# A quarter of the weights' low parts summed by accumulating DMAs from GpSimd instead of by VectorE, in a fp32 streaming-encoder block

## The chip, the core and the metric

The kernel runs on one core of one Trainium2 chip. The metric is device time of one launch, in microseconds; lower is better. The change is to be judged against the median of the runs of the kernel before, 2222.36 us.

## The reference

One layer of a hybrid encoder on 256 tokens of width 2048, all in fp32. Cut to what matters, it is a row of large projections of a few tokens:

```python
h = rms_norm(x, g_mix)
cb, cc, cv, q, k, v, g, gate_conv, gate_ret = split(h @ w_in)      # 2048 x 22528
y_conv = (cb * causal_dwconv3(cc * cv)) @ w_conv_out               # 2048 x 2048
o = head_group_norm(retention(rotary(q), rotary(k), v))            # 8 heads, chunks of 64
y_ret = (silu(g) * o) @ w_ret_out                                  # 4096 x 2048
x = x + (sigmoid(gate_conv) * y_conv + sigmoid(gate_ret) * y_ret) @ w_o
a, b = split(rms_norm(x, g_ffn) @ w_ffn_in)                        # 2048 x 11264
x = x + (silu(a) * b) @ w_ffn_out                                  # 5632 x 2048
x = x + sigmoid(rms_norm(x, g_ple) @ w_ple_gate) * (p @ w_ple_proj)
out = rms_norm(x, g_final)
```

Every weight is read once, some 416 MB in all.

## The kernel before

All projections go through one function, `project`. It takes 512 output columns at a time, for both token tiles (2 x 128 tokens), and sums over the rows of the weight in blocks of 128. Four such blocks, a group, are one load of 1 MB into a buffer `raw` ([128, 4, 512] fp32; four buffers, loads issued from SyncE). The names say which projection it is: `cc`, `cv`, `cb` (convolution), `gc`, `gr` (gates), `co`, `qk`, `v`, `g` (retention, per head), `ro`, `wo`, `fa`, `fb`, `fo` (feed-forward), `pg`, `pp`. Nearly all have 16 blocks, so 4 groups; `ro` has 8 groups, `fo` 11, `pp` a half.

To keep fp32 accuracy with the faster fp32r format, each operand is split into a high part (the value rounded to fp32r) and a low part (what the rounding left). `split` (L186) does this for a group in two halves of two blocks each, h0 = 0 and h0 = 2. For a half, ScalarE casts the raw weights into `hi` (L191) and VectorE subtracts `hi` from the raw weights into `lo` (L192). `hi` and `lo` are rings of three buffers each, so the `hi` of a half can only be written when TensorE has done all products with the third half before it. `products` (L197) then issues three matmuls for each block and token tile: high x high (L200), high x weight's low (L201), low x weight's high (L202), so 12 matmuls of 512 columns for a half:

```python
hi, lo = (pool.tile([P, 2, W], F32R, tag=g, ...) for g, x in zip(tags, ("hi", "lo")))
last_copy[0] = nc.scalar.copy(out=hi, in_=raw[:, h0 : h0 + 2, :])
nc.vector.tensor_tensor(out=lo, in0=raw[:, h0 : h0 + 2, :], in1=hi.bitcast(F32), op=ALU.subtract)
```

After a projection, ScalarE or VectorE reads its two PSUM tiles, with the activation and the row scale (for instance `sa`, the sigmoid of `fa`). Transposes for the next stage are queued by `later`, to run inside a later projection. GpSimd does almost nothing: a power for each norm (L226). The order of the instructions on each engine is set by a scheduler when the program is built; on the chip each engine runs its own queue strictly in that order.

Of the kernel before, what the change touches and what calls it, by code (L numbers as in the profile page):

```python
# [11 lines left out]
F32 = mybir.dt.float32  # L12
# [17 lines left out]
KG = 4  # L30

# columns of the combined projection
C_B, C_C, C_V = 0, D, 2 * D
# [5 lines left out]

# rows of the stacked per-feature gains, columns once transposed  # L40
G_MIX, G_FFN, G_PLE, G_CONV, G_RET = 0, 16, 32, 48, 96


def shape_constants():
    """Rotary tables [S, 2, 128] and decay masks [HEADS, 128, 384]; they depend on shapes alone."""
    f32 = np.float32
    half = DK // 2
    inv = np.power(f32(ROPE_BASE), -np.arange(half, dtype=f32) / f32(half)).astype(f32)
    ang = np.arange(S, dtype=f32)[:, None] * inv[None, :]
    rope = np.stack([np.cos(ang), np.sin(ang)], axis=1).astype(f32)  # L50
    gamma = 1.0 - 2.0 ** (-5.0 - np.arange(HEADS))
    n, m = np.arange(S)[None, :], np.arange(S)[:, None]
    decay = np.power(gamma[:, None, None], np.abs(n - m)[None].astype(np.float64))
    decay = decay * (m // CHUNK <= n // CHUNK)[None] * DK**-0.5
    masks = np.concatenate([decay[:, :P, :P], decay[:, :P, :]], axis=2).astype(f32)
    return np.ascontiguousarray(rope), np.ascontiguousarray(masks)
# [3 lines left out]
def block_kernel(  # L60
# [25 lines left out]
    const = ctx.enter_context(tc.tile_pool(name="const", bufs=1))  # L86
    blk_pool = ctx.enter_context(tc.tile_pool(name="blk", bufs=36))
    raw_pool = ctx.enter_context(tc.tile_pool(name="raw", bufs=4))
    split_pool = ctx.enter_context(tc.tile_pool(name="split", bufs=3))
    small = ctx.enter_context(tc.tile_pool(name="small", bufs=2))  # L90
    ps_mm = ctx.enter_context(tc.tile_pool(name="ps_mm", bufs=4, space=PSUM))
# [10 lines left out]

    # Work that waits for a later point of the stream of projections, so that TensorE finds its inputs ready.
    waiting = []
# [10 lines left out]

# [1 line left out]
    gains = const.tile([P, P], F32, name="gains")  # L117
# [6 lines left out]
    nc.vector.memset(minus_half, -0.5)  # L124
    # the activation table's load and TensorE's clock ramp, ahead of the data
    warm = small.tile([P, NT], F32, name="warm", bufs=1)
# [5 lines left out]
    def transposed(src, j0, name):  # L132
        """PSUM [P, 2, S]: column blocks j0 and j0 + 1 of src [P tokens, NT, ...], transposed."""
        pt = aux(name)
        for t in range(NT):
            for j in range(2):
                nc.tensor.transpose(
                    out=pt[:, j, t * P : (t + 1) * P],
                    in_=src[:, t, (j0 + j) * P : (j0 + j + 1) * P],
                    identity=ident,  # L140
                )
        return pt

    def transposed_split(src, name, gain=None, wide=W):
        """src [P tokens, NT, wide] -> high and low parts of its transpose, [P, wide // P, S] each."""
        nk = wide // P
        hi = blk([P, nk, S], F32R, f"{name}_hi")
        lo = blk([P, nk, S], F32R, f"{name}_lo")
        for j0 in range(0, nk, 2):
            pt = transposed(src, j0, f"{name}_t{j0}")  # L150
            if gain is None:
                nc.scalar.copy(out=hi[:, j0 : j0 + 2, :], in_=pt)
                nc.vector.tensor_tensor(
                    out=lo[:, j0 : j0 + 2, :], in0=pt, in1=hi[:, j0 : j0 + 2, :].bitcast(F32), op=ALU.subtract
                )
            else:
                for j in range(2):
                    g = gains[:, gain + j0 + j : gain + j0 + j + 1]
                    nc.scalar.activation(out=hi[:, j0 + j, :], in_=pt[:, j, :], func=AF.Copy, scale=g)
                    nc.vector.scalar_tensor_tensor(  # L160
                        out=lo[:, j0 + j, :],
                        in0=pt[:, j, :],
                        scalar=g,
                        in1=hi[:, j0 + j, :].bitcast(F32),
                        op0=ALU.mult,
                        op1=ALU.subtract,
                    )
        return [(hi[:, j, :], lo[:, j, :]) for j in range(nk)]

    def load(pieces, k0, kn, name, step=KG):  # L170
        """kn row blocks, from row k0 * P on, of the pieces' columns, side by side."""
        raw = raw_pool.tile([P, KG, W], F32, tag="raw", name=f"{name}_raw")
        for j in range(0, kn, step):
            at, jn = 0, min(step, kn - j)
            for w, c0, cn in pieces:
                nc.sync.dma_start(
                    out=raw[:, j : j + jn, at : at + cn],
                    in_=w[(k0 + j) * P : (k0 + j + jn) * P, c0 : c0 + cn].rearrange("(c p) n -> p c n", p=P),
                )
                at += cn  # L180
        return raw

    last_copy = [None]

    def split(raw, kn, name, pool=split_pool):
        """High and low parts of kn loaded row blocks."""  # L186
        parts = []
        for h0 in range(0, kn, 2):
            tags = ("hi", "lo") if pool is split_pool else ("blk", "blk")
            hi, lo = (pool.tile([P, 2, W], F32R, tag=g, name=f"{name}_{x}{h0}") for g, x in zip(tags, ("hi", "lo")))  # L190
# [5 lines left out]
    def products(ps, left, right, t, first, last):  # L196
        """ps += left^T @ right for token tile t, from high and low parts."""  # L197
        (xh, xl), (wh, wl) = left, right
# [5 lines left out]
    def project(lhs, nk, pieces, name, loaded=None, before=None):  # L204
        """PSUM tiles [P tokens, W], one per token tile: lhs^T @ (the pieces' columns, side by side)."""
        ps = [ps_mm.tile([P, W], F32, tag="mm", name=f"{name}_ps{t}") for t in range(NT)]
        for k0 in range(0, nk, KG):
# [3 lines left out]
            raw = load(pieces, k0, kn, name) if loaded is None else loaded[k0 // KG]  # L211
            parts = split(raw, kn, name)
            for j in range(kn):
# [5 lines left out]
    def rsqrt(r, var, scale, name, bias=EPS):  # L219
        """r = (var * scale + bias) ** -0.5: GpSimd's power, then a Newton step."""  # L220
        n = r.shape[1]
# [13 lines left out]
    class RowScale:  # L235
        """1 / rms of rows given in column chunks [P, NT, <= W]."""

# [21 lines left out]
        def so_far(self, t, n):  # L259
            """Mean square of the first n chunks of token tile t, plus EPS."""  # L260
            s = small.tile([P, 1], F32, tag="part", name="part")
# [4 lines left out]
        def done_with(self, t, n, s):  # L266
            """The scale of token tile t, from what so_far gave and chunk n, the last."""
            rsqrt(self.r[:, t : t + 1], self.parts[:, t, n : n + 1], 1.0 / D, "rms", bias=s)
            return self.r[:, t : t + 1]

# [1 line left out]
    hT = []  # L272
# [42 lines left out]

# [1 line left out]
    ycT = []  # L317
# [71 lines left out]

# [1 line left out]
    yrT = []  # L391

    def scores(h, qkT, mask):
        """High and low parts of the decayed scores, [P, 3 * P]: keys 1 with queries 1, keys 0 with queries 0 and 1."""
        sc = aux(f"sc{h}")
# [18 lines left out]
    def mix_values(h, ph, pl, vh, vl, on):  # L414
        """on = GroupNorm(scores @ v), without its gain."""
        o_ps = []
        stats = small.tile([P, NT, 2], F32, tag="stats", name=f"stats{h}")
        # (block of the scores, token tile of the keys) for the queries of each token tile
        for t, blocks in enumerate((((1, 0),), ((2, 0), (0, 1)))):
# [88 lines left out]

# [1 line left out]
    mT = []  # L510
# [11 lines left out]

# [1 line left out]
    x1, h2T = [], []  # L524
# [15 lines left out]

# [1 line left out]
    aT = []  # L542
# [38 lines left out]

# [1 line left out]
    x3 = []  # L583
# [21 lines left out]

    # the last chunk goes one token tile after the other, so that the first one's norm and store are hidden,
    # and in halves, so that little is left after the last product
    gf = blk([P, W], F32, f"gf{last}")
# [33 lines left out]
    "g_ffn", "w_ffn_in", "w_ffn_out", "g_ple", "w_ple_gate", "w_ple_proj", "g_final",  # L642
]  # fmt: skip

# [20 lines left out]
```

## Time and profile before

| what | us |
|---|---|
| runs, median of 2 (lowest, highest) | 2222.36 (2222.16, 2222.55) |
| the profiled execution: its span, first to last instruction | 2220.6 |
| TensorE busy | 2205.8 |
| VectorE busy | 1222.5 |
| ScalarE busy | 975.4 |
| GpSimd busy | 9.4 |

For the profiled execution the page gives its span and no other time; the median of the runs is 1.8 us above that span. Busy time is summed over the instructions of an engine. The engines run side by side, so the time of the kernel is that of the longest chain of instructions that wait for one another, not a sum over the engines.

### The profile page before, as it was taken

The page shows a single profiled execution, that of the slowest core. Times are in us where ns is not written, and L with a number is a line of the kernel's source. Part 1 is how long each engine was busy: PE and PEld are TensorE (multiplying, and loading weights), DVE is VectorE, ACT ScalarE, POOL GpSimd, SP SyncE. Part 2 cuts the span into 40 slices and gives each one's busy share as a digit, 9 for nine tenths or more (in the row PEclk, how much of TensorE's full clock was granted, in tenths as well). Part 3 has the DMA queues.
Part 4 walks back from the last instruction along what each step waited for, and adds up shares of the span by engine and source line. Part 5 has one row for each costly group of instructions (what it writes and reads, how often), then busy time and mean ns, then how long its engine had stood idle before and what let it go on. Part 6 is the DMA issues. An engine that isn't in the chain of part 4 may idle for free.

```text
span 2220.6 us, 24771 instructions
## 1 busy us (share of the span) xinstructions
PE 2205.8 (99%) x10054; PEld 1834.0 (83%) x10054; DVE 1222.5 (55%) x1347; ACT 975.4 (44%) x1101; POOL 9.4 (0%) x19
## 2 busy tenths in 40 slices
PE   9999999999999999999999999999999999999998
PEld 7888888888888888888888888888888888888887
DVE  5555544444666665666655555555555555444465
ACT  5444444444444444444443345444444444444454
POOL 0000000000000000000000000000000000000000
PEclk9999999999999999999999999999999999999999
DMA  7555555555555555555555565555555555555553
GB/s 263 187 189 190 189 189 190 195 199 193 174 190 182 181 179 186 178 178 180 177 190 189 190 209 205 185 190 192 191 184 191 191 190 183 196 194 191 191 195 128
DMA packets 229106, 420.05 MB, mean 189 GB/s; under 512 B 7424, under 2 KB 42368, under 8 KB 228992
## 3 DMA queue, kind: packets, MB, share of 16 engines
q1 hardware_dynamic: 228992, 418.48, 55.2%
q8 instruction: 78, 1.28, 0.2%
q14 instruction: 36, 0.29, 0.0%
HBM read 416.35 MB, written 2.10 MB: 188 GB/s over the span
## 4 chain that ended last, share of the span: by engine, by line
PE 99%; DMA 0%; ACT 0%; issue 0%; DVE 0%; SPq 0%; ACTq 0%; POOLq 0%
PE fo_ps L201 4%; PE fa_ps L202 4%; PE fa_ps L201 4%; PE fa_ps L200 4%; PE fo_ps L202 4%; PE fb_ps L200 4%; PE fo_ps L200 4%; PE fb_ps L202 4%; PE fb_ps L201 4%; PE v_ps L202 3%; PE v_ps L201 3%; PE v_ps L200 3%; PE g_ps L202 3%; PE g_ps L201 3%; PE g_ps L200 3%; PE qk_ps L201 3%
## 5 line engine op out<-in xcount | busy, mean ns | idle before, releaser
L192 DVE TENSOR_TENSOR fo_lo<-fo_raw,fo_hi 128x1024 fp32r<-128x1024 f32 x88 | 107.8, 1225 | 123.5 <-ACT fo_hi L191 123.5
L192 DVE TENSOR_TENSOR fa_lo<-fa_raw,fa_hi 128x1024 fp32r<-128x1024 f32 x88 | 107.8, 1225 | 111.4 <-ACT fa_hi L191 111.4
L192 DVE TENSOR_TENSOR fb_lo<-fb_raw,fb_hi 128x1024 fp32r<-128x1024 f32 x88 | 107.8, 1225 | 110.8 <-ACT fb_hi L191 110.8
L191 ACT CAST fa_hi<-fa_raw 128x1024 fp32r<-128x1024 f32 x88 | 92.8, 1054 | 142.8 <-PE fa_ps L202 87.9
L191 ACT CAST fo_hi<-fo_raw 128x1024 fp32r<-128x1024 f32 x88 | 92.8, 1055 | 137.4 <-PE fo_ps L202 132.4
L191 ACT CAST fb_hi<-fb_raw 128x1024 fp32r<-128x1024 f32 x88 | 92.7, 1053 | 121.9 <-PE fb_ps L202 85.3
L201 PE MATMUL fo_ps<-fo_lo,aT_hi 128*128 128x512 f32 x352 | 137.1, 389 | 0.0
L202 PE MATMUL fa_ps<-fa_hi,h2T_lo 128*128 128x512 f32 x352 | 137.0, 389 | 0.0
L201 PE MATMUL fa_ps<-fa_lo,h2T_hi 128*128 128x512 f32 x352 | 137.0, 389 | 0.0
L202 PE MATMUL fo_ps<-fo_hi,aT_lo 128*128 128x512 f32 x352 | 137.0, 389 | 0.0
L201 PE MATMUL fb_ps<-fb_lo,h2T_hi 128*128 128x512 f32 x352 | 136.9, 389 | 0.0
L202 PE MATMUL fb_ps<-fb_hi,h2T_lo 128*128 128x512 f32 x352 | 136.9, 389 | 0.0
L200 PE MATMUL fa_ps<-fa_hi,h2T_hi 128*128 128x512 f32 x352 | 127.2, 392 | 0.0
L200 PE MATMUL fo_ps<-fo_hi,aT_hi 128*128 128x512 f32 x352 | 124.4, 390 | 0.0
L192 DVE TENSOR_TENSOR ro_lo<-ro_raw,ro_hi 128x1024 fp32r<-128x1024 f32 x64 | 78.4, 1225 | 83.0 <-ACT ro_hi L191 83.0
L200 PE MATMUL fb_ps<-fb_hi,h2T_hi 128*128 128x512 f32 x352 | 122.6, 389 | 0.0
L191 ACT CAST g_hi<-g_raw 128x1024 fp32r<-128x1024 f32 x64 | 67.2, 1050 | 109.8 <-PE g_ps L202 81.9
L191 ACT CAST v_hi<-v_raw 128x1024 fp32r<-128x1024 f32 x64 | 67.4, 1054 | 106.3 <-PE v_ps L202 53.3
L192 DVE TENSOR_TENSOR v_lo<-v_raw,v_hi 128x1024 fp32r<-128x1024 f32 x64 | 78.3, 1224 | 62.4 <-ACT v_hi L191 62.4
L191 ACT CAST ro_hi<-ro_raw 128x1024 fp32r<-128x1024 f32 x64 | 67.5, 1054 | 102.3 <-PE ro_ps L202 98.9
L192 DVE TENSOR_TENSOR qk_lo<-qk_raw,qk_hi 128x1024 fp32r<-128x1024 f32 x64 | 78.3, 1224 | 61.0 <-ACT qk_hi L191 61.0
L192 DVE TENSOR_TENSOR g_lo<-g_raw,g_hi 128x1024 fp32r<-128x1024 f32 x64 | 78.3, 1224 | 60.4 <-ACT g_hi L191 60.4
(241 smaller groups left out, 5467.9 us busy)
## 6 DMA issues: line engine op xcount, KB each, us to landing
fa_raw<-in_w_ffn_in_dram SPq DMA_DIRECT2D x44, 1024.0 KB, 4.9
fb_raw<-in_w_ffn_in_dram SPq DMA_DIRECT2D x44, 1024.0 KB, 4.9
fo_raw<-in_w_ffn_out_dram SPq DMA_DIRECT2D x44, 1024.0 KB, 5.0
qk_raw<-in_w_in_dram SPq DMA_DIRECT2D x64, 512.0 KB, 4.3
v_raw<-in_w_in_dram SPq DMA_DIRECT2D x32, 1024.0 KB, 5.0
g_raw<-in_w_in_dram SPq DMA_DIRECT2D x32, 1024.0 KB, 4.8
ro_raw<-in_w_ret_out_dram SPq DMA_DIRECT2D x32, 1024.0 KB, 5.0
cv_raw<-in_w_in_dram SPq DMA_DIRECT2D x16, 1024.0 KB, 4.9
```

The source lines that it names most:

```text
L191: last_copy[0] = nc.scalar.copy(out=hi, in_=raw[:, h0 : h0 + 2, :])
L192: nc.vector.tensor_tensor(out=lo, in0=raw[:, h0 : h0 + 2, :], in1=hi.bitcast(F32), op=ALU.subtract)
L200: nc.tensor.matmul(out=ps, lhsT=xh[:, ts], rhs=wh, start=first, stop=False)
L201: nc.tensor.matmul(out=ps, lhsT=xh[:, ts], rhs=wl, start=False, stop=False)
L202: nc.tensor.matmul(out=ps, lhsT=xl[:, ts], rhs=wh, start=False, stop=last)
```

## The change

In every second group of a projection (the 2nd, 4th, ...), the second half's low part no longer comes from VectorE. ScalarE casts the high part as before, then writes its negative into a buffer `rest` (a ring of three of its own), and a DMA issued on GpSimd adds the raw weights onto it in place, from SBUF to SBUF, 512 KB each. `rest` then stands where `lo` stood. There are 190 such halves. The pool `blk`, which holds activations, goes from 36 buffers to 34 to make room. Comments are taken out as well, which moves line numbers: L191 and L192 become L201 and L202, L194 to L196 are new, and the matmuls L200 to L202 become L210 to L212.

```diff
-    blk_pool = ctx.enter_context(tc.tile_pool(name="blk", bufs=36))
+    blk_pool = ctx.enter_context(tc.tile_pool(name="blk", bufs=34))
     raw_pool = ctx.enter_context(tc.tile_pool(name="raw", bufs=4))
     split_pool = ctx.enter_context(tc.tile_pool(name="split", bufs=3))
+    rest_pool = ctx.enter_context(tc.tile_pool(name="rest", bufs=3))
...
-    def split(raw, kn, name, pool=split_pool):
+    def split(raw, kn, name, pool=split_pool, by_dma=False):
         parts = []
         for h0 in range(0, kn, 2):
+            if pool is split_pool and h0 == 2 and by_dma:
+                hi = pool.tile([P, 2, W], F32R, tag="hi", name=f"{name}_hi{h0}")
+                lo = rest_pool.tile([P, 2, W], F32R, tag="rest", name=f"{name}_rest{h0}")
+                last_copy[0] = nc.scalar.copy(out=hi, in_=raw[:, h0 : h0 + 2, :])
+                nc.scalar.activation(out=lo, in_=hi.bitcast(F32), func=AF.Copy, scale=-1.0)
+                nc.gpsimd.dma_start(out=lo, in_=raw[:, h0 : h0 + 2, :], accum_op=ALU.add)
+                parts += [(hi[:, j, :], lo[:, j, :]) for j in range(2)]
+                continue
...
-            parts = split(raw, kn, name)
+            parts = split(raw, kn, name, by_dma=k0 // KG % 2 == 1)
```

The scheduler also orders the engines' queues anew. On TensorE, at the seam between projection `fa1` and the next one, `fb1`, the queue before reads (`fa1_hi2` and `fa1_lo2` are the last half of `fa1`):

```order
L200 MATMUL fa1_ps1_10200<-fa1_hi2_10325,h2T3_hi_9916 128x512
L201 MATMUL fa1_ps1_10200<-fa1_lo2_10326,h2T3_hi_9916 128x512
L202 MATMUL fa1_ps1_10200<-fa1_hi2_10325,h2T3_lo_9917 128x512
L200 MATMUL fb1_ps0_10358<-fb1_hi0_10362,h2T0_hi_9417 128x512
L200 MATMUL fb1_ps1_10359<-fb1_hi0_10362,h2T0_hi_9417 128x512
```

`fa1` is finished before `fb1` begins. In the changed kernel, the same place on TensorE starts so (`fa1_rest2` is the low part that the DMA sums):

```order
L212 MATMUL fa1_ps1_10327<-fa1_hi0_10449,h2T3_lo_10040 128x512
L210 MATMUL fa1_ps0_10326<-fa1_hi2_10453,h2T3_hi_10039 128x512
L210 MATMUL fa1_ps1_10327<-fa1_hi2_10453,h2T3_hi_10039 128x512
L210 MATMUL fb1_ps0_10487<-fb1_hi0_10491,h2T0_hi_9534 128x512
L210 MATMUL fb1_ps1_10488<-fb1_hi0_10491,h2T0_hi_9534 128x512
```

Only the two matmuls of `fa1`'s last half that need no low part stand here; then the 12 of `fb1`'s first half follow. Still on TensorE in the changed kernel, after those 12:

```order
L211 MATMUL fb1_ps1_10488<-fb1_lo0_10492,h2T0_hi_9534 128x512
L212 MATMUL fb1_ps1_10488<-fb1_hi0_10491,h2T0_lo_9535 128x512
L211 MATMUL fa1_ps0_10326<-fa1_rest2_10454,h2T3_hi_10039 128x512
L212 MATMUL fa1_ps0_10326<-fa1_hi2_10453,h2T3_lo_10040 128x512
L211 MATMUL fa1_ps1_10327<-fa1_rest2_10454,h2T3_hi_10039 128x512
```

The other 10 matmuls of `fa1`'s last half have moved behind the first half of `fb1`. On ScalarE, the queue at the start of `fb1` before (`sa1` is the reading of `fa1`'s two PSUM tiles):

```order
L191 CAST fb1_hi0_10362<-fb1_raw_10360 128x1024
L191 CAST fb1_hi2_10366<-fb1_raw_10360 128x1024
L553 ACTIVATE sa1_10353<-fa1_ps0_10199,r2_r_9219 128x512
L553 ACTIVATE sa1_10353<-fa1_ps1_10200,r2_r_9219 128x512
L191 CAST fb1_hi0_10396<-fb1_raw_10394 128x1024
L191 CAST fb1_hi2_10400<-fb1_raw_10394 128x1024
```

The two readings stand between the first and the second group. On ScalarE in the changed kernel, the same two groups:

```order
L201 CAST fb1_hi0_10491<-fb1_raw_10489 128x1024
L201 CAST fb1_hi2_10495<-fb1_raw_10489 128x1024
L201 CAST fb1_hi0_10525<-fb1_raw_10523 128x1024
L563 ACTIVATE sa1_10482<-fa1_ps0_10326,r2_r_9334 128x512
L563 ACTIVATE sa1_10482<-fa1_ps1_10327,r2_r_9334 128x512
L194 CAST fb1_hi2_10529<-fb1_raw_10523 128x1024
L195 ACTIVATE fb1_rest2_10530<-fb1_hi2_10529 128x1024
```

The readings have moved one cast later, directly ahead of the cast and the negation of the half whose low part a DMA sums. GpSimd's queue in the feed-forward now holds nothing but these DMAs, two for each projection of four groups.

## Rows read from the trace of the kernel before

**Rows 1.** The page: span, then busy time of each engine, share, instructions.

```profile
span 2220.6 us, 24771 instructions
...
PE 2205.8 (99%) x10054; PEld 1834.0 (83%) x10054; DVE 1222.5 (55%) x1347; ACT 975.4 (44%) x1101; POOL 9.4 (0%) x19
```

**Rows 2.** The page: the chain of work that ended last, by engine.

```profile
PE 99%; DMA 0%; ACT 0%; issue 0%; DVE 0%; SPq 0%; ACTq 0%; POOLq 0%
```

**Rows 3.** Busy time by stretch: the start, the feed-forward's middle, the end.

```profile
core 0: us, PE busy (x) PEld busy (x) DVE busy (x) ACT busy (x) POOL busy (x), PEclk, DMA share, GB/s
0.00:100.00 100.00, 94.47 (x431) 78.44 (x432) 54.91 (x78) 51.84 (x75) 1.41 (x7) 0.97 0.66 228
1500.00:1800.00 300.00, 300.00 (x1354) 249.02 (x1353) 158.51 (x149) 128.20 (x134) 0.00 (x0) 1.00 0.55 189
2100.00:2221.00 121.00, 111.32 (x585) 95.91 (x583) 67.76 (x92) 56.69 (x80) 1.79 (x3) 0.98 0.48 165
```

**Rows 4.** Who waited for whom: us in total, times, longest us.

```profile
ACT fo_hi L191 <- PE fo_ps L202: 132.4, 82, 1.7
DVE fo_lo L192 <- ACT fo_hi L191: 123.5, 88, 1.5
```

**Rows 5.** Timeline around one hand-over, 1600.6 to 1604 us: PE, ACT, DVE.

```profile
start us, us, engine line op out<-in xcount [idle before <-releaser]
1600.70 0.39 PE L202 MATMUL fb_ps<-fb_hi,h2T_lo 128*128 128x512 f32 x1
1600.93 0.62 PE L200 MATMUL fa_ps<-fa_hi,h2T_hi 128*128 128x512 f32 x2
1601.13 1.06 ACT L191 CAST fa_hi<-fa_raw 128x1024 fp32r<-128x1024 f32 x1 [1.67 <-PE fb_ps L202]
1602.22 1.22 DVE L192 TENSOR_TENSOR fa_lo<-fa_raw,fa_hi 128x1024 fp32r<-128x1024 f32 x1 [0.18 <-ACT fa_hi L191]
1603.42 0.39 PE L202 MATMUL fa_ps<-fa_hi,h2T_lo 128*128 128x512 f32 x1
1603.65 0.62 PE L200 MATMUL fa_ps<-fa_hi,h2T_hi 128*128 128x512 f32 x2
1603.85 1.05 ACT L191 CAST fa_hi<-fa_raw 128x1024 fp32r<-128x1024 f32 x1 [1.66 <-PE fa_ps L202]
```

**Rows 6.** Instruction groups by form, ScalarE: count, busy us, mean ns, idle before.

```profile
L191 ACT CAST fo_hi<-fo_raw 128x1024 fp32r<-128x1024 f32 x88 | 92.8, 1055 | 137.4 <-PE fo_ps L202 132.4 <-PE fb_ps L202 5.0
...
L553 ACT ACTIVATE sa<-fa_ps,r_r 128x512 f32<-128x512 f32 x22 | 15.1, 690 | 10.8 <-PE fa_ps L202 10.8
...
L347 ACT CAST ych<-y 128x512 fp32r<-128x512 f32 x8 | 4.9, 622 | 0.4
...
L635 ACT ACTIVATE x<-x,r_r 128x512 f32<-128x512 f32 x4 | 2.7, 715 | 2.8 <-DVE r_r L233 2.8
```

**Rows 7.** The page's costliest groups: the subtraction on VectorE.

```profile
L192 DVE TENSOR_TENSOR fo_lo<-fo_raw,fo_hi 128x1024 fp32r<-128x1024 f32 x88 | 107.8, 1225 | 123.5 <-ACT fo_hi L191 123.5
```

**Rows 8.** DMA issues: count, KB each, median us from issue to landing.

```profile
fa_raw<-in_w_ffn_in_dram SPq DMA_DIRECT2D x44, 1024.0 KB, 4.9
...
cc_raw<-in_w_in_dram SPq DMA_DIRECT2D x8, 512.0 KB, 9.8
res<-in_x_dram SPq DMA_DIRECT2D x4, 512.0 KB, 6.0
pp_raw<-in_w_ple_proj_dram SPq DMA_DIRECT2D x4, 512.0 KB, 3.6
...
mix_in<-in_g_mix_dram SPq DMA_DIRECT2D x1, 8.0 KB, 1.7
```

## The prediction

> **What bounds the kernel now.** I read the page's busy times first: TensorE is busy 2205.8 of 2220.6 us, VectorE 1222.5, ScalarE 975.4 [rows 1]. The chain that ended last is 99% TensorE [rows 2], and by stretch TensorE has no gap at all in the middle (300.00 of 300 us at granted clock 1.00); its 14.8 us of idle time lie at the start and the end [rows 3]. So the kernel is bound by its matmuls. VectorE and ScalarE run ahead and then wait for TensorE to free a `hi` buffer: 82 of the 88 casts of `fo` wait for that, 1.7 us at most, and the subtraction waits for the cast [rows 4]. Taking work from VectorE shortens nothing on the path. It can only show where TensorE was idle, so even a perfect result is worth less than 14.8 us, 0.7%; what a measurement of this kernel tells from no change is about 2%, 44 us. The question is whether the new way of making a low part is ready in time, since from a TensorE that never waits, each wait is added to the end in full.
>
> How much time is there? The timeline of one hand-over shows it [rows 5]. Twelve matmuls, one half, take 1603.65 - 1600.93 = 2.72 us, 0.2265 each. The last matmul with an old half starts at 1600.70, its slot ends at 1600.93; the cast starts 0.20 later, takes 1.06, the subtraction starts 0.03 later and takes 1.22. So a low part is there 0.20 + 1.06 + 0.03 + 1.22 = 2.5 us after its buffer came free. TensorE wants it two halves and two matmuls later, 26 x 0.2265 = 5.9 us: 3.4 us to spare now.
>
> **The change part by part.**
>
> *Removed:* 190 subtractions of 1.225 us [rows 7], 233 us of VectorE. All of it lies beside TensorE's work: worth nothing.
>
> *Added on ScalarE:* 190 negations of 1024 columns. No row has one. The cast of that size takes 1.055; a scaled copy of 512 columns takes 0.715 against 0.622 for a cast of 512 from the same memory [rows 6]. So between 1.05 and 2 x 0.715 = 1.43; I take the cast plus the difference, 1.15. That is 219 us on an engine with 1245 us free, again nothing in sum, but each stands in the chain of its low part.
>
> *Added:* 190 accumulating DMAs of 512 KB. Call L the time from the issue on GpSimd to the landing that TensorE waits for. The chain is now 0.20 + 1.06 + 0.03 + 1.15 + 0.03 = 2.5 us, and then L. Each place has its own slack for L:
> - At the end of a projection the scheduler puts the first half of the next one in front (shown in the order of the change): 38 matmuls instead of 26, 8.6 us, slack 6.1. The 77 projections of four groups and the four `ro` end so: 81 places.
> - The other 109 are inside projections. Where nothing else is ahead on ScalarE the slack is 5.9 - 2.5 = 3.4: 64 places (`fo`, most of `ro`, `fa`, `v`, `g`, `cb`).
> - The half moved behind the next projection's first half frees its buffer late. In the next four-group projection ScalarE's queue has the cast that needs this buffer ahead of the cast for the DMA, so the count begins there: 3.4 - 1.06 = 2.3. I count 22 such places (`qk`, `cc`, `gc`, `wo`, `pg`).
> - Where ScalarE also reads the finished PSUM tiles in between, two of 0.69 us [rows 6], 2.3 - 1.4 leaves 1.0: 23 places (`fb`, `gr`, `co`, `cv`), as the order of ScalarE shows for `fb1`.
>
> A wait in one place does not shorten the next, since the count starts from TensorE's own progress. So the added time is 81 (L - 6.1) + 64 (L - 3.4) + 22 (L - 2.3) + 23 (L - 1.0), each term only where it is positive.
>
> *L.* The trace has no DMA from GpSimd, none that adds and none inside SBUF. Below: a plain load of 512 KB lands 3.6 us after its issue (`pp_raw`), and 8 KB, almost no data, takes 1.7. Above: 512 KB among a pile of loads at the start takes 9.8 (`cc_raw`), and `res`, 512 KB issued into the stream, 6.0 [rows 8]. An adding DMA must read both operands, 1 MB in all, and 1 MB lands in 4.9 (`fa_raw`, rows 8). The weight stream also goes on: it holds the DMA engines for 0.55 of the time [rows 3], that is 0.55 x 5.44 = 3.0 us for each group of 5.44, and a DMA that comes at any moment shares with it for about 0.55 x 3.0 = 1.6 us. I take 4.9 + 1.6 = 6.5, near the row of `res`, and keep 3.6 and 9.8 as ends. The descriptor work on GpSimd has no row; it is inside this spread.
>
> The Trainium skill speaks against the change here. Its page "Collectives: The Full Stack", section "The bandwidth ceiling: the fold count and why AG ≠ RS ≠ AR", says that a reduction in a DMA reads two sources through one read ring and so runs at half the rate of a copy. No row here shows an adding DMA; by that rule the plain 3.6 us is no fair price, and the sum would be the one made from the 1 MB row.
>
> Sum at L = 6.5: 81 x 0.4 = 32, 64 x 3.1 = 198, 22 x 4.2 = 92, 23 x 5.5 = 127, together 450 us. On the profiled execution that is 2220.6 + 450 = 2670.6; the median of the runs lies 1.8 above the span, so **2672 us**, 20% slower. At L = 3.6 the sum is 101 and the time 2324; at 9.8 it is 1077 and 3299.
>
> *Edits that I cost at nothing.* The raw buffer of every second group is held until the DMA has read it, so its next load starts later; there are four buffers, 21.8 us of TensorE work, for a load of 4.9 us, and if a stall of 6 us is added it still lands in time. VectorE's other work comes earlier, not later. `blk` loses two of 36 buffers; they are needed only where heads and gates are all held, late in the retention, and a shortage would cost waits of a few us there. The DMAs share GpSimd's queue with 13 powers that wait for VectorE; one DMA stands behind each, and if it came late that is 13 waits of a few us at most. Stalls leave TensorE idle in short gaps; at the start, where it idles 5.5 of 100 us, the granted clock is 0.97 [rows 3], so I price no clock loss.
>
> **The rivals.**
>
> *Quick as a plain copy* (L between 2.6 and 4.3). If adding costs no more than copying and the stream does not disturb it, L is 3.6 and the time 2324. For it: the DMA engines are idle 45% of the time, and nothing goes to HBM. Against: `res` took 6.0 for the same bytes. The Trainium skill, page "DMA: Bandwidth & Descriptors", section "Anatomy of one DMA — SWDGE (gpsimd) path", fits 2.0 us plus bytes over 436 GB/s, an estimate of 3.2 us for 512 KB, which would give 70 us and 2293; it is a fit for copies, and no run here shows it.
>
> *Hidden* (not slower). Where L is 2.6 or less the sum is 22 x 0.3 + 23 x 1.6 = 43 us, within 2%; at 2.3 it is 30 us, 2252. It needs an adding DMA of 512 KB to beat every load of that size in the trace by a us, against a floor of 1.7 for 8 KB. TensorE's waits in the `fb` places would then be the only ones.
>
> *The DMA becomes the bound* (L over 8.5). If the adding path is slow in the DMA engines, or GpSimd takes microseconds to issue, all 190 waits lengthen together, 190 us for each us of L: 3052 at 8.5, 3299 at 9.8, and beyond that the weight loads come late too. For it: nothing in the trace shows the rate of adding. Against: 45% of the DMA time is free.
>
> **How the numbers follow.** Forecast, L from 4.3 to 8.5: 0.72. Quick copy: 0.11. DMA as the bound: 0.13. Hidden: 0.04, of which 0.01 for a gain over 2%, which needs an unseen saving on TensorE. The range goes from L = 3.6 to L = 8.5, 2324 to 3052, and I write 2325 to 3050; it leaves out some 0.07 below and 0.13 above. Slower by over 2%: 0.95, within: 0.04, faster: 0.01.
>
> **What would show it.** TensorE's waits should name the DMA of `rest`, in about 190 places, with L read as issue to landing near 6.5; TensorE's busy time should stay near 2200 while the span grows; VectorE should fall by 233 us and ScalarE rise by 219. The waits at the seams (81) should be under 1 us and those in `fb` and `gr` the longest, near 5.5. The forecast is wrong if L is under 4.3, if waits name loads or `lo` instead, or if the longer time comes with longer matmuls or a lower clock.

## The result and the profile after

The changed kernel takes 2401.05 us (two runs, 2399.01 and 2403.08) against 2222.36: a ratio of 1.0805, 95% interval 1.0773 to 1.0836. It is slower, as forecast, and inside the range, but by 179 us and not by 450. The profiled execution grew from a span of 2220.6 to 2401.3 us, 180.7 us.

The page of the changed kernel, against [rows 1] and [rows 2]:

```profile
span 2401.3 us, 25606 instructions
...
PE 2257.7 (94%) x10054; PEld 1843.6 (77%) x10054; DVE 996.2 (41%) x1157; ACT 1173.1 (49%) x1291; POOL 176.8 (7%) x209
...
q0 software_dynamic: 27360, 99.63, 22.0%
...
issue 81%; PE 12%; DMA 4%; ACT 1%; POOL 1%; DVE 1%; POOLq 0%; SPq 0%; ACTq 0%
```

VectorE fell by 226 us and ScalarE rose by 198, both beside the path. TensorE's idle time went from 14.8 to 2401.3 - 2257.7 = 143.6 us, 129 more, and its busy time rose by 52. These two are the whole 181 us. Do not read the chain here: 81% of it is put down to "issue", time in which the engine waited for nothing that the profile shows. The waits name the cause at once.

The waits of TensorE in the changed kernel (us in total, times, longest), where the kernel before had none in the stream:

```profile
PE fo_ps L211 <- DMA fo_rest<-fo_raw: 21.6, 19, 1.3
PE fb_ps L211 <- DMA fb_rest<-fb_raw: 20.4, 11, 2.1
PE ro_ps L211 <- DMA ro_rest<-ro_raw: 14.6, 12, 1.9
PE qk_ps L211 <- DMA qk_rest<-qk_raw: 12.4, 8, 2.3
PE co_ps L211 <- DMA co_rest<-co_raw: 7.7, 4, 2.2
PE gr_ps L211 <- DMA gr_rest<-gr_raw: 7.4, 4, 1.9
PE fa_ps L211 <- DMA fa_rest<-fa_raw: 7.0, 11, 1.9
PE cv_ps L211 <- DMA cv_rest<-cv_raw: 6.7, 4, 1.8
PE v_ps L211 <- DMA v_rest<-v_raw: 6.6, 8, 1.8
```

All rows of waits for `rest`, fourteen, are together 127 us in 100 waits. None of TensorE's waits names a load. `fa`, `fb`, `qk` and `v` have two DMAs in each projection, but wait in only half as many places: 11 of 22, 11 of 22, 8 of 16, 8 of 16. The half at the seam, moved behind the next projection's first half, does not wait.

One wait of `fb`, in the timeline of the changed kernel (start, duration, engine):

```profile
1696.89 1.05 ACT L201 CAST fb_hi<-fb_raw 128x1024 fp32r<-128x1024 f32 x1 [2.12 <-PE fb_ps L212]
...
1698.48 1.37 ACT L563 ACTIVATE sa<-fa_ps,r_r 128x512 f32<-128x512 f32 x2 [0.53 <-PE fa_ps L212]
...
1699.74 1.04 ACT L194 CAST fb_hi<-fb_raw 128x1024 fp32r<-128x1024 f32 x1
1700.81 1.06 ACT L195 ACTIVATE fb_rest<-fb_hi 128x1024 fp32r<-128x1024 f32 x1
...
1702.28 0.87 POOL L196 DMA_DIRECT2D fb_rest<-fb_raw  x1 [10.58 <-ACT fb_rest L195]
...
1704.40 0.61 PE L210 MATMUL fb_ps<-fb_hi,h2T_hi 128*128 128x512 f32 x2
...
1706.87 0.50 PE L211 MATMUL fb_ps<-fb_rest,h2T_hi 128*128 128x512 f32 x1 [1.85 <-DMA fb_rest<-fb_raw]
1707.20 0.40 PE L212 MATMUL fb_ps<-fb_hi,h2T_lo 128*128 128x512 f32 x1
```

The negation ends at 1701.87, GpSimd begins 0.41 us later, and 4.6 us after that, at 1706.87, the low part can be read. The first matmul after the wait also holds its slot for 0.33 us (1706.87 to 1707.20) instead of 0.23. And the wait in the list begins at the modelled end of the last matmul, 0.16 us after its slot ended. So a listed wait costs TensorE about 0.26 us more than its row says; over all 100 waits of the trace it is the same on average.

The DMA issues of the changed kernel (KB each, median us from issue to landing), against [rows 8]:

```profile
fa_raw<-in_w_ffn_in_dram SPq DMA_DIRECT2D x44, 1024.0 KB, 6.1
...
fa_rest<-fa_raw POOLq DMA_DIRECT2D x22, 512.0 KB, 4.6
fb_rest<-fb_raw POOLq DMA_DIRECT2D x22, 512.0 KB, 4.5
fo_rest<-fo_raw POOLq DMA_DIRECT2D x20, 512.0 KB, 4.5
```

L, the time from the issue to the landing, is 4.5 to 4.7 us in every projection (median of the 190: 4.55), not 6.5.

### The profile page after: what moved, and what is told of

The parts are those of the page before. It is cut to its first block, busy times and chain, and to the rows that moved or that the text cites. A ratio compares the mean times of both kernels' runs of the same rounds, so it can differ in the third digit from the quotient of the medians.

```text
span 2401.3 us, 25606 instructions
## 1 busy us (share of the span) xinstructions
PE 2257.7 (94%) x10054; PEld 1843.6 (77%) x10054; DVE 996.2 (41%) x1157; ACT 1173.1 (49%) x1291; POOL 176.8 (7%) x209
## 4 chain that ended last, share of the span: by engine, by line
issue 81%; PE 12%; DMA 4%; ACT 1%; POOL 1%; DVE 1%; POOLq 0%; SPq 0%; ACTq 0%
PE v_ps L211 2%; DMA v_rest<-v_raw 2%; PE v_ps L212 2%; PE v_ps L210 1%; PE g_ps L210 1%; PE g_ps L212 1%; PE g_ps L211 1%; PE sc L411 0%; DMA fo_rest<-fo_raw 0%; DMA fo_raw<-in_w_ffn_out_dram 0%; PE o L434 0%; DMA cc_rest<-cc_raw 0%; DVE g_lo L202 0%; PE pg L211 0%; PE pg L212 0%
## 5 line engine op out<-in xcount | busy, mean ns | idle before, releaser
L202 DVE TENSOR_TENSOR fo_lo<-fo_raw,fo_hi 128x1024 fp32r<-128x1024 f32 x68 | 83.3, 1226 | 175.2 <-ACT fo_hi L201 175.1
L202 DVE TENSOR_TENSOR fb_lo<-fb_raw,fb_hi 128x1024 fp32r<-128x1024 f32 x66 | 80.9, 1226 | 172.9 <-ACT fb_hi L201 172.9
L212 PE MATMUL fb_ps<-fb_hi,h2T_lo 128*128 128x512 f32 x352 | 139.9, 398 | 0.0
L212 PE MATMUL fa_ps<-fa_hi,h2T_lo 128*128 128x512 f32 x352 | 138.8, 394 | 0.0
L212 PE MATMUL fo_ps<-fo_hi,aT_lo 128*128 128x512 f32 x352 | 137.4, 390 | 0.0
L202 DVE TENSOR_TENSOR fa_lo<-fa_raw,fa_hi 128x1024 fp32r<-128x1024 f32 x66 | 80.9, 1225 | 134.4 <-ACT fa_hi L201 133.0
L210 PE MATMUL fo_ps<-fo_hi,aT_hi 128*128 128x512 f32 x352 | 126.7, 390 | 0.0
L210 PE MATMUL fb_ps<-fb_hi,h2T_hi 128*128 128x512 f32 x352 | 126.4, 395 | 0.0
L201 ACT CAST fo_hi<-fo_raw 128x1024 fp32r<-128x1024 f32 x68 | 71.5, 1052 | 110.5 <-PE fo_ps L212 104.3
L201 ACT CAST fb_hi<-fb_raw 128x1024 fp32r<-128x1024 f32 x66 | 69.5, 1053 | 114.6 <-PE fb_ps L212 90.0
L210 PE MATMUL fa_ps<-fa_hi,h2T_hi 128*128 128x512 f32 x352 | 125.2, 391 | 0.0
L202 DVE TENSOR_TENSOR ro_lo<-ro_raw,ro_hi 128x1024 fp32r<-128x1024 f32 x48 | 58.8, 1226 | 123.4 <-ACT ro_hi L201 123.4
L201 ACT CAST fa_hi<-fa_raw 128x1024 fp32r<-128x1024 f32 x66 | 69.6, 1055 | 78.8 <-PE fa_ps L212 29.0
L211 PE MATMUL fo_ps<-fo_lo,aT_hi 128*128 128x512 f32 x272 | 105.8, 389 | 0.0
L202 DVE TENSOR_TENSOR qk_lo<-qk_raw,qk_hi 128x1024 fp32r<-128x1024 f32 x48 | 58.8, 1225 | 106.6 <-ACT qk_hi L201 106.6
L211 PE MATMUL fa_ps<-fa_lo,h2T_hi 128*128 128x512 f32 x264 | 103.0, 390 | 0.0
L211 PE MATMUL fb_ps<-fb_lo,h2T_hi 128*128 128x512 f32 x264 | 103.0, 390 | 0.0
L212 PE MATMUL qk_ps<-qk_hi,hT_lo 128*128 128x512 f32 x256 | 101.1, 395 | 0.0
L212 PE MATMUL ro_ps<-ro_hi,yrT_lo 128*128 128x512 f32 x256 | 100.3, 392 | 0.0
L212 PE MATMUL v_ps<-v_hi,hT_lo 128*128 128x512 f32 x256 | 99.9, 390 | 0.0
L212 PE MATMUL g_ps<-g_hi,hT_lo 128*128 128x512 f32 x256 | 99.8, 390 | 0.0
L202 DVE TENSOR_TENSOR v_lo<-v_raw,v_hi 128x1024 fp32r<-128x1024 f32 x48 | 58.8, 1226 | 96.6 <-ACT v_hi L201 96.6
```

Of the source, the lines that this page charges most:

```text
L210: nc.tensor.matmul(out=ps, lhsT=xh[:, ts], rhs=wh, start=first, stop=False)
L211: nc.tensor.matmul(out=ps, lhsT=xh[:, ts], rhs=wl, start=False, stop=False)
L212: nc.tensor.matmul(out=ps, lhsT=xl[:, ts], rhs=wh, start=False, stop=last)
```

## The experiments

Each is an edit of the changed kernel, unless it says otherwise, and is compared with the kernel before on the same chip (2220.7 to 2222.1 us). Only the plain copy and the half weight stream keep the order of every queue of the changed kernel, and the fewer activation buffers that of the kernel before; in the others the scheduler orders the queues anew, so that these runs differ in more than the edit shown.

**Four buffers for the high parts.** Does the lead alone decide? (The `hi` of the halves without DMA has four buffers as well.)

```diff
-    rest_pool = ctx.enter_context(tc.tile_pool(name="rest", bufs=3))
+    rest_pool = ctx.enter_context(tc.tile_pool(name="rest", bufs=2))
...
-                hi = pool.tile([P, 2, W], F32R, tag="hi", name=...)
+                hi = pool.tile([P, 2, W], F32R, tag="hi", name=..., bufs=4)
```

> The changed kernel with four buffers for the high parts instead of three (and two instead of three for rest, so that the room is the same). All 190 adding DMAs stay. Theory 1 (the low part lands later than TensorE wants it, nothing else): a fourth buffer gives each chain 12 matmuls, 2.7 us, more; inside projections the slack for the DMA goes from about 3 to 5.8 us, over the 4.55 us that it takes, so TensorE's waits for rest fall from 125 us to under 15, its busy time comes back to about 2206, the half-clock stretches inside the stream go, and the time is 2222 to 2240. Theory 2 (the DMAs also slow TensorE or the loads by their traffic): the waits go but 40 to 50 us of longer busy time stay, 2265 or more.

Measured: 2326.2 us, ratio 1.0462 (1.0445 to 1.048). Theory 1's range is missed by 86 us. Theory 2's, 2265 or more, holds the time, but not for its reason: the waits did not go. TensorE's waits in this run:

```profile
PE fb_ps L211 <- DMA fb_rest<-fb_raw: 20.1, 11, 2.1
PE gr_ps L211 <- DMA gr_rest<-gr_raw: 8.1, 4, 2.1
...
PE fa_ps L211 <- DMA fa_rest<-fa_raw: 7.8, 11, 1.8
...
PE qk_ps L211 <- DMA qk_rest<-qk_raw: 1.4, 1, 1.4
...
PE fo_ps L211 <- DMA fo_rest<-fo_raw: 0.5, 1, 0.5
```

In `fo` and `qk` the fourth buffer does what theory 1 says: from 21.6 to 0.5 us, and from 12.4 to 1.4. In `fb`, `gr`, `co` and `cv`, where ScalarE reads finished PSUM tiles first, the wait stays; they have 43.8 of the 74.9 us that are left. The timeline of `fb` here shows why:

```profile
1563.86 1.37 ACT L563 ACTIVATE sa<-fa_ps,r_r 128x512 f32<-128x512 f32 x2 [2.57 <-PE fa_ps L212]
...
1565.13 1.04 ACT L194 CAST fb_hi<-fb_raw 128x1024 fp32r<-128x1024 f32 x1
1566.07 1.05 ACT L201 CAST fb_hi<-fb_raw 128x1024 fp32r<-128x1024 f32 x1
1567.02 1.05 ACT L195 ACTIVATE fb_rest<-fb_hi 128x1024 fp32r<-128x1024 f32 x1
...
1568.48 0.87 POOL L196 DMA_DIRECT2D fb_rest<-fb_raw  x1 [12.93 <-PE fb_ps L212]
```

ScalarE idles 2.57 us for TensorE to finish `fa`, with the cast for the DMA queued behind that reading. A buffer that is free earlier is of no use to an instruction that stands behind another one's wait. `fa` keeps its waits too, though ScalarE reads no PSUM tiles ahead of its DMA; why was not tried. Against theory 2, TensorE's busy time fell from 2257.7 to 2235.3 along with the waits.

**A plain copy instead of an add.** What does the add itself cost?

```diff
-                nc.gpsimd.dma_start(out=lo, in_=raw[:, h0 : h0 + 2, :], accum_op=ALU.add)
+                nc.gpsimd.dma_start(out=lo, in_=raw[:, h0 : h0 + 2, :])
```

> The changed kernel with the same 190 DMAs as plain copies: the low part becomes the raw weights, the sum is left out. The order of all queues stays. If adding costs more than copying because two operands are read (the step in the prediction), the DMA falls from 4.55 us to about 3.6, and 97 waits get 0.95 us shorter each: about 2300 us. If the add is free, it stays at 4.5 us and the time at 2400.

Measured: 2242.14 us in one run, against 2300 expected for a copy of 3.6 us. The copy takes 2.9, and the waits for `rest` fall to 6.7 us:

```profile
q0 software_dynamic: 27360, 99.63, 12.4%
...
fo_rest<-fo_raw POOLq DMA_DIRECT2D x20, 512.0 KB, 2.9
```

The order is the same and so is the number of DMAs, so 1.65 us less from issue to landing is worth 159 of the 179 us. The new order, the negations and the smaller `blk` together can have cost no more than the 20 us that are left. The queue's share gives the work in the DMA engines: an add holds all 16 for 0.220 x 2401.3 / 190 = 2.78 us, a copy of the same bytes for 0.124 x 2240.4 / 190 = 1.46. The ratio is 1.9, and 2.78 is near the 3.0 us that 1 MB of loads takes. Here the Trainium skill, page "Collectives: The Full Stack", section "The bandwidth ceiling: the fold count and why AG ≠ RS ≠ AR", agrees with the run: between a collective that copies and one that reduces it gives a measured ratio of 1.93, and puts it down to the two source reads of the reduction.

**Half the weight stream.** Does sharing with the loads lengthen the add?

```diff
-            raw = load(pieces, k0, kn, name) if loaded is None else loaded[k0 // KG]
+            raw = load(pieces, k0, min(2, kn), name) if loaded is None else loaded[k0 // KG]
```

with both halves then made from the first two blocks.

> The changed kernel loads only the first two of each group's four blocks and uses them for both halves, so half of the weights are left out; every other instruction and the order stay. If sharing with the weight stream is a part of the DMA's 4.55 us (1.6 us in the prediction), half a stream takes 0.8 us or more away: 3.7 us, and about 2320 us in all. If the time of the DMA is issue, adding and landing alone, it stays within 0.2 us of 4.55 and the time within 25 us of 2400.

Measured: 2386.64 us, and the add takes the same:

```profile
q1 hardware_dynamic: 123520, 219.25, 28.3%
q0 software_dynamic: 27360, 99.63, 22.1%
...
fo_rest<-fo_raw POOLq DMA_DIRECT2D x20, 512.0 KB, 4.5
```

With half the loads gone L stays at 4.5 us in `fo`, and falls by no more than 0.2 us in any projection (the median of the 190 goes from 4.55 to 4.54). The reason is in the changed kernel itself, in its stretches around the DMA of the timeline above:

```profile
core 0: us, PE busy (x) PEld busy (x) DVE busy (x) ACT busy (x) POOL busy (x), PEclk, DMA share, GB/s
1698.00:1702.00 4.00, 4.00 (x19) 3.30 (x19) 2.63 (x3) 3.49 (x5) 0.00 (x0) 1.00 1.05 403
1702.30:1703.20 0.90, 0.90 (x5) 0.74 (x5) 0.24 (x1) 0.63 (x1) 0.85 (x1) 1.00 0.09 30
...
1704.00:1706.00 2.00, 1.01 (x5) 0.51 (x3) 0.52 (x2) 1.05 (x1) 0.00 (x0) 1.00 1.05 201
```

Before the add, loads fill the DMA engines at 403 GB/s; while GpSimd is at work on its DMA instruction they are nearly idle; then the add fills them alone, at 201 GB/s. Adds and loads take turns. A wait on SyncE's queue is behind it, as its waits (us in total, times, longest), its issues and GpSimd's in the timeline show:

```profile
SPq L177 <- DMA fb_rest<-fb_raw: 244.3, 22, 13.0
...
1690.83 0.87 POOL L196 DMA_DIRECT2D fa_rest<-fa_raw  x1 [11.57 <-ACT fa_rest L195]
...
1695.52 0.37 SPq L177 DMA_DIRECT2D fb_raw<-in_w_ffn_in_dram  x1
1696.06 11.82 SPq L177 DMA_DIRECT2D fa_raw<-in_w_ffn_in_dram  x3
```

The add issued at 1690.83 lands about 4.6 us later, and two loads are issued soon after, at 1695.52 and 1696.06. The first needs the raw buffer that the add was reading. The second stands behind it in the queue, but its own buffer too was free only at 1696.0, when VectorE had read it. All 190 adds are waited for so by a load. Counted over the DMA packets of the trace, in 97% of the 190 adds the loads take less than 5% of the DMA engines' time while the add's data moves.

**VectorE adds instead of the DMA.** Does the negation on ScalarE cost anything?

```diff
-                nc.gpsimd.dma_start(out=lo, in_=raw[:, h0 : h0 + 2, :], accum_op=ALU.add)
+                nc.vector.tensor_tensor(out=lo, in0=raw[:, h0 : h0 + 2, :], in1=lo.bitcast(F32), op=ALU.add)
```

> The changed kernel with ScalarE's negation kept, but VectorE adds the raw weights onto it, no DMA. The chain is then 0.2 + 1.06 + 1.06 + 1.23 us, 3.6 us, against 5.9 us of lead inside a projection. Theory 1: no waits for the low part, 2222 to 2235 us. Rival (the longer ScalarE queue, with 190 negations, makes the high parts late): waits for hi or lo, 2250 or more.

Measured: 2221.55 us, the time of the kernel before, with ScalarE busy 1175.5 us and no wait for `lo` or `hi` in the stream. In this run's order the 190 negations cost nothing, and neither does a chain of one more microsecond.

**Fewer activation buffers alone.** The kernel before with `blk` at 34.

```diff
-            parts = split(raw, kn, name, by_dma=k0 // KG % 2 == 1)
+            parts = split(raw, kn, name, by_dma=False)
```

> The kernel before with the pool of activations at 34 buffers instead of 36 and no DMA, no negation. The prediction cost this at nothing: 2222 within 6 us. If the two buffers matter, TensorE waits late in the retention and the time is over 2230.

Measured: 2222.52 us. Nothing, as the prediction had it.

**Half the bytes in each add.**

```diff
-                nc.gpsimd.dma_start(out=lo, in_=raw[:, h0 : h0 + 2, :], accum_op=ALU.add)
+                nc.gpsimd.dma_start(out=lo[:, 0:1, :], in_=raw[:, h0 : h0 + 1, :], accum_op=ALU.add)
```

> The changed kernel with each adding DMA over the first of its two blocks only, 256 KB (the second block's low part stays the negated high part, so that part of the sum is left out). The prediction's base, that an add takes the time of a load of both operands, gives 1.65 us less for half the bytes at the slope that copy and add show (2.9 and 4.55 us for 512 KB): about 3.3 us from issue to landing. If an add has a fixed price whatever its size, it stays over 4.2.

Measured: 3.3 us from issue to landing in every projection, and 2247.51 us. That is the 3.3 expected, but not by its working: 1.65 us less would have been 2.9. So 256 KB of adding costs 4.55 - 3.3 = 1.25 us. By a straight line through the two sizes, an estimate, 2.0 us are left at no bytes, of which GpSimd is busy 0.88. (The order is another here, so the time is not to be compared place by place; L is.) Almost no wait is listed, and yet 27 us are lost. The timeline shows where:

```profile
1601.52 0.61 PE L210 MATMUL fb_ps<-fb_hi,h2T_hi 128*128 128x512 f32 x2
1602.26 0.47 PE L211 MATMUL fb_ps<-fb_rest,h2T_hi 128*128 128x512 f32 x1
1602.57 0.39 PE L212 MATMUL fb_ps<-fb_hi,h2T_lo 128*128 128x512 f32 x1
```

The two matmuls from 1601.52 should give way at 1601.97; the next one starts at 1602.26 and holds its slot for 0.31. That is 0.37 us lost and only 0.13 us of it uncovered, too short to be listed: small waits vanish under the modelled ends of matmuls. Counted over the starts of all matmuls in this trace, the step onto a `rest` and the slot after it lose 17 + 6 of the 27 us.

**Two adds, one after the other.** The dose raised.

```diff
                 nc.gpsimd.dma_start(out=lo, in_=raw[:, h0 : h0 + 2, :], accum_op=ALU.add)
+                nc.gpsimd.dma_start(out=lo, in_=raw[:, h0 : h0 + 2, :], accum_op=ALU.add)
```

> The changed kernel with a second adding DMA onto the same low part after the first (the raw weights are added twice, so the sum is another). The time from the negation to the low part grows by one more issue and landing, about 4.9 us. If the waits come from that time alone, all 109 places inside projections wait 4.9 us longer and the seams, whose slack the prediction put at 6.1, begin to wait for about 9.4 - 6 = 3 us where the order there stays: 500 to 800 us more than the changed kernel, 2900 to 3200. If the waits come from something else in the change (ScalarE's queue, the loads), the time grows far less, under 2600.

Measured: 3304.65 us, more than either theory. TensorE's idle time is 642 us above that of the changed kernel, within the 500 to 800; its busy time is 259 above, which I had not counted. The page, busy times and granted clock:

```profile
PE 2516.8 (76%) x10054; PEld 2014.0 (61%) x10054; DVE 999.8 (30%) x1157; ACT 1177.2 (36%) x1291; POOL 343.3 (10%) x399
...
PEclk8889988888989898888777898898889977777878
```

A stretch of one wait of 11 us in `fo` in the same run:

```profile
core 0: us, PE busy (x) PEld busy (x) DVE busy (x) ACT busy (x) POOL busy (x), PEclk, DMA share, GB/s
...
2923.00:2926.00 3.00, 0.00 (x0) 0.00 (x0) 0.00 (x0) 0.00 (x0) 0.00 (x0) 0.50 0.98 280
```

In this stretch TensorE stands still and is granted 0.50 of its clock, 1.2 GHz instead of 2.4. The second add and the loads that waited for the first meet here: 280 GB/s, between the 201 of an add and the 403 of loads, and that add lands 9 us after its issue instead of 4.55. So where the two meet, sharing does lengthen the add.

**The DMA later in the projection, with four buffers.** The negations moved away from the PSUM readings; an edit of the kernel with four buffers.

```diff
-            parts = split(raw, kn, name, by_dma=k0 // KG % 2 == 1)
+            parts = split(raw, kn, name, by_dma=k0 // KG % 4 >= 2)
```

> As the run with four high-part buffers, but the DMA makes the low part in the 3rd and 4th group of every four instead of the 2nd and 4th; the number stays 190. ScalarE's queue has the readings of the finished PSUM tiles in the 2nd group, so no negation stands behind them any more. Theory 1a (what was left with four buffers, 90 us of idle TensorE, comes from ScalarE's queue, where casts for the DMA stand behind those readings): TensorE's waits for rest fall under 25 us and the time is 2225 to 2255. Theory 1b (what is left is the DMA and its queue on GpSimd, wherever the place): waits of about 1.8 us stay in some 45 places, 2290 or more.

Measured: 2268.1 us, ratio 1.0223 (1.0197 to 1.0249). The rows of waits for `rest` sum to 26 us, a little over the 25 of theory 1a, and `fb` has 2.0 us in 4 waits instead of 20.1 in 11. The time is 13 us over its range. L has become longer, 5.0 to 6.5 us by projection, and adds now meet loads: only in 44% of them do the loads take less than 5% of the DMA engines' time. I put that down to two groups in a row that hold their raw buffers, so that the loads that follow run into the next add.

**The same place with three buffers.**

> The changed kernel with the DMA in the 3rd and 4th group of every four, and three high-part buffers as in the change: the place alone, without the fourth buffer. If the buffers set the lead, every place inside a projection has the slack that fo shows, about 3.1 us, against 4.55: 109 waits of about 1.5 us and their refill, 2370 to 2410. If what mattered was ScalarE's queue behind the readings of PSUM, the place alone gives most of the gain and the time is under 2320.

Measured: 2460.8 us, slower than the changed kernel and above both ranges. Two groups in a row, with L at 4.6 to 6.8 us, wait in 139 places. In `fa`, a first add has the DMA engines alone, at 193 GB/s in the stretch of its middle, and the second, issued at 1715.69, meets a load, 346 GB/s, and lands 9 us later:

```profile
1713.50:1714.50 1.00, 0.07 (x1) 0.00 (x0) 0.00 (x0) 0.97 (x2) 0.00 (x0) 1.00 1.03 193
...
1718.60:1719.60 1.00, 1.00 (x6) 0.84 (x5) 0.25 (x1) 0.72 (x1) 0.00 (x0) 1.00 1.01 346
```

So in these runs the place helps only together with the lead, and moving it has a price of its own in the DMA engines. No run with the DMA beats the kernel before; TensorE has 14.8 us of idle time there, and nothing here takes matmuls away.

## Why the prediction was right in kind and wrong in size

- **What bounds the kernel: right.** TensorE had no slack. The 226 us taken off VectorE gained nothing in any run, and ScalarE's added work costs nothing where VectorE adds: that run takes as long as the kernel before.
- **The mechanism: right.** The low part lands after TensorE wants it, in 100 places; at L = 6.5 it would have been all 190. With the order unchanged, the plain copy shortens that by 1.65 us and gives back 159 of 179 us.
- **L, the step that failed.** I took 4.9 + 1.6 = 6.5. The first part, a load of both operands, was near: 4.55 alone in the DMA engines, 2.78 us of their time against 1.46 for a copy. The second, 1.6 us for sharing with the stream, was an average over any moment, and the add does not come at any moment: loads wait for it on SyncE's queue. The range for L, 3.6 to 9.8, held the value. At L = 4.6, GpSimd's start to TensorE's, the prediction's own sum is 64 x 1.2 + 22 x 2.3 + 23 x 3.6 = 210 us instead of 450. So the term that was mis-sized is the sharing, 1.6 us: half the stream gone took nothing off L, and without the term the sum would have been 243. The base, 4.9 against 4.55, is the rest of it.
- **The slack of 3.4 us and of 6.1: right within the hand-over to GpSimd.** `fo` waits 21.6 / 19 = 1.1 us, 1.3 with the hidden 0.16, so its slack is 3.3. Others of the 64 places wait less, `fa` 0.6, and `g` not at all; there transposes or matmuls of the retention stand in between on TensorE, which I had not counted. The seams, at 6.1, do not wait at all. GpSimd begins 0.4 us after the negation, not 0.03; the negation took 1.06, not 1.15.
- **The slack of 1.0 and 2.3 us: too small.** `fb`, `gr`, `co` and `cv` wait 42 us in 23 places, 2.0 us each with the hidden part, not 3.6; the slack is 2.6. `qk`, `cc`, `gc`, `wo` and `pg` wait 34 us in 23 places, 1.6 each so, not 2.3. I had taken the high parts' buffers as a strict ring of three. In the timeline the cast at 1696.89 goes as soon as `fb`'s own first half is done, while the last half of `fa`, whose buffer it should need in a ring, is still being read. So that cast is out of the way before the PSUM readings. This is read from the trace, not tried by itself.
- **Left out: the price of waiting.** The 100 waits cost 0.26 us each beyond their rows, 26 us. Thirteen stretches of 3.4 us at half clock lie inside the stream, about 22 us. With the 127 us of waits that is 175 of the 181 us. I had priced no clock loss, from the granted clock at the start, and had named a lower clock as a sign against me: 52 of the 181 us did come as longer busy time of TensorE.
- **Luck.** That the sum at the right L, 210, is near 181 is in part luck: the waits came out some 70 us below it, and what I had left out added some 40.

One stretch with such a drop in the changed kernel, and one without:

```profile
1500.00:1520.00 20.00, 18.14 (x73) 14.46 (x72) 8.04 (x8) 8.62 (x9) 0.87 (x1) 0.91 0.79 238
...
1680.00:1700.00 20.00, 19.60 (x91) 16.02 (x90) 9.07 (x10) 9.88 (x12) 0.87 (x1) 1.00 0.73 214
```

In the first, TensorE had waited 1.86 us for `fb_rest`; 1.3 us after it went on, its matmuls went from 0.23 to 0.43 us apart for eight of them. 73 were done in these 20 us, 91 in the other.

## What to carry to other kernels

Where an engine is never idle, price a replacement by its latency, not by the work it takes off others: count the lead that the buffers and each in-order queue leave, and set the time from issue to landing against it. An adding DMA inside SBUF cost the DMA engines here 1.9 times what a copy of the same bytes costs, and by the estimate from two sizes 2.0 us besides; 512 KB of it did not fit into 3 us of lead. A deeper ring did not help where the instruction that needs it stands behind another one's wait.

## What the runs showed that I had not expected

- An add of 512 KB takes 4.55 us, a copy 2.9, an add of 256 KB 3.3. GpSimd is busy 0.88 us for an add and 0.54 for a copy, and starts 0.4 us after ScalarE's result.
- Adds and loads took turns, though only a load's wait for its buffer orders them: 403 GB/s, then 201. Where two adds followed each other the turns broke, and an add took up to 9 us.
- The granted clock fell to 0.50 for 3.4 us at some waits of 1.2 to 2.6 us, in 13 places in the changed kernel, and in over 100 places with two adds. There TensorE's busy time is 311 us above that of the kernel before, together with the refill after each wait. Which waits bring it about was not settled.
